# One more step in the ramp of a channel shuffle: tiles of 4, 8, 16, 24 KB a partition instead of 4, 8, 16, and 12 KB last instead of 4

## Chip, cores and metric

The kernel runs on one core of one Trainium2 chip. The metric is device time in microseconds. A run's state is fast unless it is over 1.5% above the fastest run of the same kernel; all comparisons below are between fast runs.

## The reference

```python
batch, h, w, c = 16, 64, 64, 256;  groups = 8
x = x.reshape(batch, h, w, groups, c // groups)
x = x.transpose(0, 1, 2, 4, 3)
x = x.reshape(batch, h, w, c)          # float32
```

Within each run of 256 channels an 8 x 32 matrix is transposed. Nothing is calculated: 67.1 MB are read and 67.1 MB are written.

## The kernel before

```python
_SIZES = [4, 8, 16] + [32] * 15 + [4]     # pixels a partition; one pixel is 1 KB
_IN_BUFS = 3
_OUT_BUFS = 3
...
first = 0
for q in _SIZES:
    in_tile = in_pool.tile([P, biggest * c], F32, name="in_tile")
    nc.sync.dma_start(out=in_tile[:, : q * c], in_=rows(x_flat, first, q))
    out_tile = out_pool.tile([P, biggest * c], F32, name="out_tile")
    nc.vector.tensor_copy(
        out=out_tile[:, : q * c].rearrange("p (i j g) -> p i j g", j=CPG, g=G),
        in_=in_tile[:, : q * c].rearrange("p (i g j) -> p i j g", g=G, j=CPG),
    )
    nc.scalar.dma_start(out=rows(out_flat, first, q), in_=out_tile[:, : q * c])
    first += P * q
```

A tile of q KB a partition is one contiguous piece of 128 q KB in HBM, one row of q KB for each partition. Loads go out from the sync queue, stores from the scalar queue; VectorE does the shuffle between them. Load number k + 3 is issued when copy k is done, since there are three input buffers.

## Time and profile before

| | before |
|---|---|
| time, median of fast runs | 316.9 us |
| profiled span | 315.2 us |
| DMA engines' packet time | 99.2% of 16 engines' span |
| VectorE busy | 119.9 us, 38% |
| one 32 KB row on one DMA engine | 1213 ns |
| period of a 32 KB tile in the middle | 19.4 us, of which the copy 7.5 |

The prediction below shows the lines that this table comes from. Two more things help to read them. The first is how deep the queues are. The page's DMA issues of the kernel before give output and input, engine, count, KB and the median time from issue to landing:

```profile
in_tile<-in_x_dram SPq DMA_DIRECT2D x15, 4096.0 KB, 50.5
out_dram<-out_tile ACTq DMA_DIRECT2D x15, 4096.0 KB, 42.4
```

A 4 MB transfer takes 8 rows x 1213 ns = 9.7 us of each engine, but lands 50 or 42 us after its issue. The rest is waiting behind other rows. The second is the copy of the first 32 KB tile in the timeline (start, duration, engine, what it does, and in brackets how long the engine had been idle and for what):

```profile
24.38 7.50 DVE L49 COPY out_tile<-in_tile 128x8192 f32<-128x8192 f32 x1 [7.81 <-DMA in_tile<-in_x_dram]
```

VectorE stands idle for 7.81 us where the tiles jump from 16 to 32 KB. This is the gap that the change aims at.

### The profile page before, as it was taken

What the parts mean: (1) busy time and instruction counts of PE and PEld (TensorE: products, weight loads), DVE (VectorE), ACT (ScalarE), POOL (GpSimd) and SP (SyncE); (2) the same over time, 40 slices, a digit from 0 to 9 for tenths busy, and PEclk for the clock granted to TensorE, in tenths of its full rate; (3) what the DMA queues carried; (4) which work ended last, traced back from release to release, by engine and by line L of the source; (5) the groups of instructions that cost most, each with busy time, mean ns of one, the idle gap of its engine ahead of it and who ended that gap; (6) DMA issues with size and microseconds to landing.
All of it is one profiled execution on the core that took longest, in us unless ns stands there. A gap on an engine that the chain in (4) does not pass through costs nothing.

```text
span 315.2 us, 150 instructions
## 1 busy us (share of the span) xinstructions
DVE 119.9 (38%) x19; POOL 0.2 (0%) x4
## 2 busy tenths in 40 slices
DVE  2419270905318062270722608135090440905500
POOL 0000000000000000000000000000000000000000
DMA  8999999999999999999999999999999999999996
GB/s 314 408 422 458 403 449 408 457 408 453 412 453 412 458 412 453 420 445 428 437 428 437 437 428 437 428 437 433 437 433 437 428 441 424 445 420 426 439 441 291
DMA packets 5472, 134.22 MB, mean 426 GB/s; under 512 B 608, under 2 KB 608, under 8 KB 1120
## 3 DMA queue, kind: packets, MB, share of 16 engines
q1 hardware_dynamic: 2736, 67.11, 49.8%
q10 hardware_dynamic: 2736, 67.11, 49.4%
HBM read 67.11 MB, written 67.11 MB: 426 GB/s over the span
## 4 chain that ended last, share of the span: by engine, by line
DMA 40%; another core or an unknown queue 30%; DVE 25%; issue 0%; DVEq 0%; SPq 0%
DMA in_tile<-in_x_dram 40%; DVE out_tile L49 25%; DVEq L49 0%; SPq L47 0%
## 5 line engine op out<-in xcount | busy, mean ns | idle before, releaser
L49 DVE COPY out_tile<-in_tile 128x8192 f32<-128x8192 f32 (+3 forms) x19 | 119.9, 6313 | 179.3 <-DMA in_tile<-in_x_dram 179.3
L71 POOL MEMSET const-uint8-127<- 128x1 uint8 x1 | 0.1, 103 | 0.0
L71 POOL MEMSET const-bfloat16-1.0<- 128x1 bf16 x1 | 0.1, 102 | 0.0
L71 POOL MEMSET const-float32-0.0<- 128x1 f32 x1 | 0.1, 99 | 0.2 <-issue 0.2
L71 POOL MEMSET const-float32-1.0<- 128x1 f32 x1 | 0.1, 99 | 0.0
## 6 DMA issues: line engine op xcount, KB each, us to landing
in_tile<-in_x_dram SPq DMA_DIRECT2D x15, 4096.0 KB, 50.5
out_dram<-out_tile ACTq DMA_DIRECT2D x15, 4096.0 KB, 42.4
in_tile<-in_x_dram SPq DMA_DIRECT2D x1, 2048.0 KB, 11.1
out_dram<-out_tile ACTq DMA_DIRECT2D x1, 2048.0 KB, 30.1
in_tile<-in_x_dram SPq DMA_DIRECT2D x2, 512.0 KB, 22.7
in_tile<-in_x_dram SPq DMA_DIRECT2D x1, 1024.0 KB, 5.5
out_dram<-out_tile ACTq DMA_DIRECT2D x2, 512.0 KB, 14.4
out_dram<-out_tile ACTq DMA_DIRECT2D x1, 1024.0 KB, 22.9
```

Source lines behind the costliest of these rows:

```text
L49: nc.vector.tensor_copy(out=out_tile[:, : q * c].rearrange("p (i j g) -> p i j g", j=CPG, g=G), in_=in_tile[:, : q * c].rearrange("p (i g ...
L71: nc = _bacc.Bacc("TRN2", target_bir_lowering=False, num_devices=1)
```

## The change

The intent: a step of 24 KB between 16 and 32 KB, so that the fourth tile is loaded, copied and stored sooner. To keep the total at 512 KB a partition, one 32 KB tile goes, and the last tile grows from 4 to 12 KB. Nothing else changes, and there are still nineteen tiles.

```diff
-_SIZES = [4, 8, 16] + [32] * 15 + [4]
+_SIZES = [4, 8, 16, 24] + [32] * 14 + [12]
```

## The prediction

> **What bounds the kernel now.** I read the page first: how full the DMA engines are, and what each queue's packets took.
>
> ```profile
> span 315.2 us, 150 instructions
> ...
> DVE 119.9 (38%) x19; POOL 0.2 (0%) x4
> ...
> DMA packets 5472, 134.22 MB, mean 426 GB/s; under 512 B 608, under 2 KB 608, under 8 KB 1120
> ...
> q1 hardware_dynamic: 2736, 67.11, 49.8%
> q10 hardware_dynamic: 2736, 67.11, 49.4%
> ```
>
> The two queues (q1 loads, q10 stores) together fill 49.8 + 49.4 = 99.2% of sixteen engines' span: 0.992 x 315.2 = 312.7 us of packet time per engine. VectorE, the only other worker, is busy 38%. So the engines' packet time is the bound, and what a change can win without cutting it is the other 0.8%, about 2.5 us. The windows say where that sits (columns: stretch and length, VectorE busy, GpSimd busy, clock, DMA share, GB/s; a packet is put wholly into the stretch in which it starts, so a share may pass 1.00).
>
> ```profile
> 0.00:2.00 2.00, 0.00 (x0) 0.20 (x4) 1.00 0.18 29
> 2.00:16.00 14.00, 6.39 (x3) 0.00 (x0) 1.00 1.00 404
> 16.00:32.00 16.00, 8.07 (x2) 0.00 (x0) 1.00 1.04 442
> 32.00:74.00 42.00, 14.89 (x2) 0.00 (x0) 1.00 1.00 431
> 74.00:287.00 213.00, 82.03 (x11) 0.00 (x0) 1.00 1.00 433
> 287.00:312.00 25.00, 8.55 (x2) 0.00 (x0) 1.00 0.99 426
> 312.00:313.90 1.90, 0.00 (x0) 0.00 (x0) 1.00 0.64 261
> 313.90:315.15 1.25, 0.00 (x0) 0.00 (x0) 1.00 0.00 0
> ```
>
> Idle engine time: 2.0 x 0.82 = 1.6 us before the first packet, 1.9 x 0.36 = 0.7 us while the engines finish one by one, 1.25 us after the last packet. In between, through ramp, middle and drain, there is no hole: the share is 0.99 to 1.04 in every stretch. (The three add up to 3.6 us, not 2.5, because neighbouring packet records overlap by a few ns.)
>
> Third, what the change could touch: the copies by shape, and VectorE's waits.
>
> ```profile
> L49 DVE COPY out_tile<-in_tile 128x8192 f32<-128x8192 f32 x15 | 111.9, 7459 | 166.2 <-DMA in_tile<-in_x_dram 166.2
> L49 DVE COPY out_tile<-in_tile 128x4096 f32<-128x4096 f32 x1 | 3.8, 3835 | 4.1 <-DMA in_tile<-in_x_dram 4.1
> L49 DVE COPY out_tile<-in_tile 128x1024 f32<-128x1024 f32 x2 | 2.2, 1099 | 7.6 <-DMA in_tile<-in_x_dram 7.6
> L49 DVE COPY out_tile<-in_tile 128x2048 f32<-128x2048 f32 x1 | 2.0, 2019 | 1.5 <-DMA in_tile<-in_x_dram 1.5
> ```
>
> All of VectorE's idle time waits for loads. The timeline of the end:
>
> ```profile
> 287.23 7.47 DVE L49 COPY out_tile<-in_tile 128x8192 f32<-128x8192 f32 x1 [11.95 <-DMA in_tile<-in_x_dram]
> 294.73 4.92 ACTq L53 DMA_DIRECT2D out_dram<-out_tile  x2
> 298.20 1.09 DVE L49 COPY out_tile<-in_tile 128x1024 f32<-128x1024 f32 x1 [3.50 <-DMA in_tile<-in_x_dram]
> ```
>
> The last copy ends at 299.29 us, but packets run until 313.9: 14.6 us of stores are still queued. The chain of waits stops at that last copy, so the chain isn't what sets the end here; the backlog is.
>
> **What the skill says.** (1) "DMA: Bandwidth & Descriptors", section "Issuing engines are not separate DMA queues": transfers issued from different engines run on the same 16 DMA engines and interleave. The trace agrees: two queues at 49.8% and 49.4%, never both full. (2) Same page, "Queues, rings and completion order": each engine goes round its queues packet by packet. The packet records agree, row by row: over 287 to 297 us one engine alternates a 4 KB load row (159 ns) with a 32 KB store row (1213 ns). (3) Same page, "Where 436 GB/s comes from": a ceiling of 435.2 GB/s. The middle runs at 433, so there is half a per cent to be had by any arrangement of transfers. (4) "SBUF — State Buffer", "SBUF: two separate sides": a compute instruction cannot slow a DMA. The records agree: the 32 KB store rows' median and 95th percentile are both 1213 ns, VectorE busy or not.
>
> **The change, part by part.** Row records by size: 4 KB 159 ns, 8 KB 309, 16 KB 611, 32 KB 1213, and a 9 ns packet for each transfer's semaphore. From 16 to 32 KB that is 602/16 = 37.6 ns a KB, so I put 24 KB at 611 + 8 x 37.6 = 912 ns and 12 KB at 309 + 4 x 37.7 = 460 ns (estimates by interpolation). Each engine moves 8 rows of a tile.
>
> Removed, each direction: one 32 KB tile and one 4 KB tile, 8 x (1213 + 159) = 10.98 us. Added: 24 KB and 12 KB, 8 x (912 + 460) = 10.98 us. Net 0.00. The tiles stay nineteen, the packets 5472, the bytes 134.22 MB.
>
> VectorE: removed 7.46 + 1.10 = 8.56 us. Added, at (7459 - 3835)/16 = 227 ns a KB: 24 KB 3.84 + 1.81 = 5.65, 12 KB 2.02 + 0.91 = 2.93, together 8.58. Net +0.02 us, on an engine with 62% idle.
>
> Ramp: the first three loads are the same, and the fourth is still issued at the end of the first copy, 5.2 us. The 32 KB load landed at 24.3 and its copy ended at 31.9. A 24 KB load has 8 x (1213 - 912) = 2.4 us less ahead of it, so lands near 21.9; its copy of 5.65 ends near 27.6. So fourth store and seventh load go out 4.3 us earlier. Does an engine have nothing else to do in that time? Before, the load of the sixth tile, issued at 16.6, landed only at 54.7, and the third store, issued at 16.6, only at 46.7: both queues hold work past 31.9. An earlier issue only lengthens a queue. Worth 0.
>
> Drain: before the last load can be finished, 8 KB a row less has to be loaded than before, and stores keep pace, so the last 32 KB load lands 2 x 8 rows x 8 KB x 37.6 ns = 4.8 us earlier, 287.15 - 4.8 = 282.3. The last load's 12 KB rows alternate with 32 KB store rows: 8 x (460 + 1213) = 13.4 us (before 8 x (159 + 1213) = 11.0, and the two loads landed 10.9 apart), so it lands near 295.7. Copy 2.93 and about 0.1 of issue: store out near 298.8, about 1.0 us to its first packet (as at the start, 0.73 to 1.76). The queue before it holds stores until 313.9 - 8 x 0.46 = 310.2. Slack 310.2 - 299.8 = 10.4 us, against 313.9 - 1.3 - 300.3 = 12.3 before. Still hidden.
>
> Sum: 0.00 engine time, 0 at the start (same first load), 0 at the end. Span 315.2, time 316.9.
>
> **Rivals.** First: the ramp step pays. If the 4.3 us of earlier store filled a hole, the time would be 316.9 - 4.3 = 312.6, faster by 1.4%. For it: a jump from 16 to 32 KB looks coarse, and VectorE does wait 7.8 and 6.0 us after it. Against: the share in 2 to 32 us is 1.00 to 1.04, so there is no hole; VectorE's idleness costs nothing. Second: the larger last tile is exposed: its copy is 1.8 us longer and its store 8 x (460 - 159) = 2.4 us longer, together +4.2, time 321.1, slower by 1.3%. For it: that is what a last tile does where nothing else is queued, and the chain ends on it. Against: 10.4 us of slack. Third: rows of 24 and 12 KB run worse than interpolated, or the start has more slow packets. In the first 20 us, packet records exceed their usual duration by 0.9 us per engine in all; should the regrouped ramp double or drop this, the time moves by up to 0.9 us either way. If the new sizes were 10% slow, 2 x 10.98 x 0.1 = +2.2 us. No sign of it: cost is linear over the four sizes seen. None of the rivals alone crosses 2% (6.3 us).
>
> **Range and chances.** The best number is the time before, 316.9. Its three runs span 0.7 us (316.57 to 317.26); with the slow packets of the ramp and a small step between sessions I take 0.8 us either side: 316.1 to 317.7. A change over 2% needs a hole that no view shows, or a mechanism that I've not thought of: 1% each way; within 2%, 98%.
>
> **What would show it.** Right: the queues still add up to about 99.2%, packets are 5472, the share in every stretch from 2 to 312 us is 0.99 or more, the fourth copy takes about 5.65 us and ends near 27.6, the last copy takes about 2.9 and ends near 298.7, and packets end near 313.9. Wrong: a stretch in 2 to 32 us under 0.97 (ramp), a last store that lands well after the one ahead of it by more than its own 3.7 us (drain), or 24 KB rows well away from 912 ns (packet cost). A time under 315 or over 319 would mean that the sum of packet time isn't what sets the end.

## The result

The changed kernel takes 316.80 us (316.57 to 316.97, six runs), the kernel before in the same rounds 316.91 us (316.57 to 317.26, six runs). The ratio is 0.9997, with a 95% interval of 0.9984 to 1.001: no difference. Ratios here are the mean time of one kernel's fast runs over that of the other's of the same rounds, so not quite the ratio of the medians quoted.

The page of the changed kernel:

```profile
span 314.8 us, 150 instructions
...
DVE 120.4 (38%) x19; POOL 0.2 (0%) x4
...
DMA packets 5473, 134.22 MB, mean 426 GB/s; under 512 B 609, under 2 KB 609, under 8 KB 865
...
q1 hardware_dynamic: 2736, 67.11, 49.8%
q10 hardware_dynamic: 2736, 67.11, 49.4%
```

The two queues have the same packets, bytes and shares as before. (The one packet more is of a third queue, which fetches instructions.) The windows:

```profile
2.00:16.00 14.00, 6.54 (x3) 0.00 (x0) 1.00 1.00 408
16.00:32.00 16.00, 6.11 (x2) 0.00 (x0) 1.00 1.00 426
32.00:74.00 42.00, 19.52 (x3) 0.00 (x0) 1.00 1.02 437
74.00:287.00 213.00, 82.44 (x12) 0.00 (x0) 1.00 1.00 434
287.00:312.00 25.00, 5.79 (x2) 0.00 (x0) 1.00 0.98 421
```

No hole appeared, none closed. (The trace also has one record for each DMA packet, with its start, duration, size and queue; "packet records" means these. In them the engines are full up to 310 us; the 0.98 comes from rows put into the stretch in which they start.) The copies of the new shapes, and the timelines of ramp and end:

```profile
L49 DVE COPY out_tile<-in_tile 128x6144 f32<-128x6144 f32 x1 | 5.7, 5651 | 5.5 <-DMA in_tile<-in_x_dram 5.5
...
L49 DVE COPY out_tile<-in_tile 128x3072 f32<-128x3072 f32 x1 | 3.0, 2976 | 6.0 <-DMA in_tile<-in_x_dram 6.0
```

```profile
21.98 5.65 DVE L49 COPY out_tile<-in_tile 128x6144 f32<-128x6144 f32 x1 [5.52 <-DMA in_tile<-in_x_dram]
35.52 7.51 DVE L49 COPY out_tile<-in_tile 128x8192 f32<-128x8192 f32 x1 [7.89 <-DMA in_tile<-in_x_dram]
```

```profile
282.39 7.43 DVE L49 COPY out_tile<-in_tile 128x8192 f32<-128x8192 f32 x1 [11.88 <-DMA in_tile<-in_x_dram]
295.79 2.98 DVE L49 COPY out_tile<-in_tile 128x3072 f32<-128x3072 f32 x1 [5.97 <-DMA in_tile<-in_x_dram]
```

The fourth copy ends at 27.6 instead of 31.9 us, and the last copy ends at 298.8 instead of 299.3. VectorE's longest idle stretch in the ramp has moved one tile on (7.89 us ahead of the fifth copy) and isn't shorter. The last packet ends at 313.4 us (before: 313.9). So the intended effect is there, 4.3 us, and the time does not see it.

### The profile page after: what moved, and what is told of

Same layout as the page of the kernel before. It is cut to its first block, busy times and chain, and to the rows that moved or that the text cites. A ratio compares the mean times of both kernels' runs of the same rounds, so it can differ in the third digit from the quotient of the medians.

```text
span 314.8 us, 150 instructions
## 1 busy us (share of the span) xinstructions
DVE 120.4 (38%) x19; POOL 0.2 (0%) x4
## 3 DMA queue, kind: packets, MB, share of 16 engines
q1 hardware_dynamic: 2736, 67.11, 49.8%
q10 hardware_dynamic: 2736, 67.11, 49.4%
## 4 chain that ended last, share of the span: by engine, by line
DMA 44%; another core or an unknown queue 26%; DVE 24%; issue 0%; SPq 0%; DVEq 0%
DMA in_tile<-in_x_dram 44%; DVE out_tile L49 24%; SPq L47 0%; DVEq L49 0%
## 5 line engine op out<-in xcount | busy, mean ns | idle before, releaser
L49 DVE COPY out_tile<-in_tile 128x8192 f32<-128x8192 f32 (+5 forms) x19 | 120.4, 6336 | 178.4 <-DMA in_tile<-in_x_dram 178.4
## 6 DMA issues: line engine op xcount, KB each, us to landing
out_dram<-out_tile ACTq DMA_DIRECT2D x1, 3072.0 KB, 31.9
```

Of the source, the lines that this page charges most:

```text
L49: nc.vector.tensor_copy(out=out_tile[:, : q * c].rearrange("p (i j g) -> p i j g", j=CPG, g=G), in_=in_tile[:, : q * c].rearrange("p (i g ...
```

## The experiments

**Theory:** from about 2 to 310 us every DMA engine always has a row to move; the sum of the row times sets the end, and the change leaves it alone. **Rival 1:** the ramp step gains up to 4.3 us and the larger last tile loses as much. **Rival 2:** VectorE's chain sets the end, and the change happens to be neutral in it.

The diffs are cut to the lines that matter. They are taken against the changed kernel; where only a new `_SIZES` line stands, it replaces the changed kernel's.

### The ramp step alone

```diff
-_SIZES = [4, 8, 16, 24] + [32] * 14 + [12]
+_SIZES = [4, 8, 16, 24] + [32] * 14 + [8, 4]
```

> The ramp step alone: 4, 8, 16, 24 KB, fourteen of 32, then 8 and 4 KB, so the last tile is the old 4 KB. Main theory (the DMA engines are never without work between start and drain, so the sum of row times sets the end): 316.8 us plus at most 0.5 for one more small tile, ratio to before 0.999 to 1.003. Rival that the ramp step gains up to 4.3 us and the larger last tile gives it back: about 312.6 us, ratio 0.986.

Measured: 316.82 us against 316.69, ratio 1.0004 (0.9992 to 1.0017). With the old last tile back (and one tile of 8 KB before it, so twenty tiles), the ramp step still gains nothing.

### The 24 KB tile at the end instead of in the ramp

```diff
-_SIZES = [4, 8, 16, 24] + [32] * 14 + [12]
+_SIZES = [4, 8, 16] + [32] * 14 + [24, 12]
```

> The same nineteen tile sizes as the changed kernel, with the 24 KB tile moved from the ramp to the place before the last: 4, 8, 16, fourteen of 32, 24, 12 KB. Main theory: 316.8 us, ratio 0.998 to 1.002, as the rows are the same and the order doesn't matter. Rival that ramp step and last tile are worth +-4 us and cancel: the ramp gain is taken away and the larger last tile kept, about 321 us, ratio 1.013.

Measured: 316.69 us against 316.69, ratio 0.9999 (0.9985 to 1.0012). The larger last tile without the ramp step costs nothing. With the run before, this rules out rival 1: two parts that are each worth nothing cannot be a gain and a loss that cancel.

### Every copy done twice

```diff
+        for _ in range(2):
             nc.vector.tensor_copy(...)
```

> The changed kernel with every copy done twice, VectorE busy 241 us instead of 120 and a 32 KB copy 15 us against a period of 19.4. Main theory: VectorE is not on the path; 316.8 us, up to 319 because the drain's slack falls (last copy 6 us instead of 3, and the one before it 15 instead of 7.5). Rival that the chain of waits (copies are 24 per cent of it) sets the end: 75 us more, about 390 us.

Measured: 317.02 us, ratio 1.0008 (0.9995 to 1.002). The 32 KB copies of the changed kernel, and of this one:

```profile
L49 DVE COPY out_tile<-in_tile 128x8192 f32<-128x8192 f32 x14 | 104.8, 7484 | 157.4 <-DMA in_tile<-in_x_dram 157.4
```

```profile
L50 DVE COPY out_tile<-in_tile 128x8192 f32<-128x8192 f32 x28 | 209.7, 7491 | 52.6 <-DMA in_tile<-in_x_dram 52.0
```

VectorE's busy time doubled from 120.4 to 240.9 us; its idle time before these copies fell from 157.4 to 52.6 us. It paid from its idleness. Rival 2 is out, though copies make up 24% of the chain of waits. Each copy of that chain is followed by a wait, put down to a load or to "another core or an unknown queue" (26% of the span); such a chain names what the copies wait for, not what a longer copy would cost.

### How much slack has the ramp? The 24 KB copy three and eight times

```diff
+        for _ in range(3 if q == 24 else 1):      # and 8
             nc.vector.tensor_copy(...)
```

> The changed kernel with the copy of its 24 KB tile (the fourth, the one the change put in) done three times: its store and the seventh load go out 11.3 us later, 38.9 instead of 27.6 us. Main theory: the third store occupies the store queue to 42 us and the loads of the fifth and sixth tile the load queue to about 46 us, so no engine runs dry: 316.8 us, ratio 0.998 to 1.003. Rival that the ramp's timing is on the path: up to 328 us.

Measured: 316.68 us against 316.63, ratio 0.9998 (0.9981 to 1.0015). The copy by shape:

```profile
L50 DVE COPY out_tile<-in_tile 128x6144 f32<-128x6144 f32 x3 | 17.0, 5667 | 5.5 <-DMA in_tile<-in_x_dram 5.5
```

The fourth tile was held back by 17.0 - 5.7 = 11.3 us, more than twice what the change had brought it forward, and nothing came of it.

> The same copy done eight times: it ends near 67 us and the seventh load and fourth store reach the engines near 68. Main theory: the two loads still queued are done near 46 us, so the engines stand still for about 22 us and the time grows by that: 337 to 341 us, with a visible hole from 46 to 68 us. If the ramp had no slack at all the growth would be the whole 39.6 us, 356 us; if it grows by nothing, the main theory is wrong.

Measured: 340.27 us, 23.6 more than before (ratio 1.0747). The copy by shape, and the windows with the hole:

```profile
L50 DVE COPY out_tile<-in_tile 128x6144 f32<-128x6144 f32 x8 | 45.7, 5718 | 5.7 <-DMA in_tile<-in_x_dram 5.5
```

```profile
40.00:46.00 6.00, 5.97 (x2) 0.00 (x0) 1.00 1.11 481
46.00:68.00 22.00, 21.90 (x5) 0.00 (x0) 1.00 0.00 0
68.00:74.00 6.00, 6.00 (x2) 0.00 (x0) 1.00 0.92 306
```

The copies added 45.7 - 5.65 = 40.1 us (39.6 was expected); 22 us of DMA idleness followed, and another 1.3 us per engine of slow load rows when work came back (in the packet records, between 60 and 80 us). So a hole does cost its length, and the method would have seen one. The ramp has some 18 us of slack before the engines run dry (40.1 less the hole of 22), or 16.5 by the time (40.1 less the 23.6 that showed, slow rows included).

### How much slack has the end? The last copy four and eight times

```diff
+        for _ in range(4 if q == 12 else 1):      # and 8
             nc.vector.tensor_copy(...)
```

> The changed kernel with the copy of its last tile (12 KB) done four times, 8.9 us longer: the last store is issued near 307.7 and reaches the engines near 308.8, while the store before it keeps them until 309.4 to 309.8. Main theory: hidden, 316.8 us, ratio 0.998 to 1.003. Rival that the last tile's copy and store are exposed (chain of waits ends there): 325.7 us.

Measured: 316.70 us against 316.63, ratio 1.0 (0.9985 to 1.0015). Hidden: 8.9 us of extra copying cost nothing.

> The last copy done eight times, 20.8 us longer. Main theory: the drain's slack is 309.6 minus 299.8, about 9.8 us, so 20.8 - 9.8 = 11.0 us show: 327.8 us (326.5 to 329). Rival that it is exposed from the start: 337.6 us.

Measured: 327.73 us (median; one of four runs, 331.2, lifts the ratio to 1.0375). That is 11.1 us more than the 316.63 us of before. The timeline and the windows of its end:

```profile
295.86 23.91 DVE L50 COPY out_tile<-in_tile 128x3072 f32<-128x3072 f32 x8 [5.82 <-DMA in_tile<-in_x_dram]
```

```profile
300.00:309.00 9.00, 8.90 (x4) 0.00 (x0) 1.00 1.05 451
309.00:321.00 12.00, 10.67 (x4) 0.00 (x0) 1.00 0.04 16
321.00:325.80 4.80, 0.00 (x0) 0.00 (x0) 1.00 0.68 287
```

The copies end 23.91 - 2.98 = 20.9 us later, 11.1 show, so the last tile had 20.9 - 11.1 = 9.8 us of slack behind the stores of the tiles ahead of it.

### No ramp at all: a miss

```diff
-_SIZES = [4, 8, 16, 24] + [32] * 14 + [12]
+_SIZES = [32] * 16
```

> No ramp at all, sixteen tiles of 32 KB. Main theory: the three loads issued at the start are 29 us of work for the engines, the first copy ends near 19.5 us, so no engine runs dry in the ramp; three tiles fewer save about 0.4 us of small packets; the last copy of 7.5 us and its issue eat nearly all of the backlog of one 32 KB store (9.7 us), so up to 1 us may be lost there. 316 to 318 us. Rival that a ramp is needed because the first store waits: the first store goes out near 19.5 instead of 5.2 us, so up to 14 us more, 331 us.

Measured: 324.33 us (323.27 to 325.15) against 316.69, ratio 1.0238 (1.022 to 1.0257). Neither number was right. The windows:

```profile
74.00:287.00 213.00, 81.27 (x11) 0.00 (x0) 1.00 1.00 423
287.00:304.00 17.00, 4.01 (x2) 0.00 (x0) 1.00 1.00 432
304.00:312.00 8.00, 4.57 (x1) 0.00 (x0) 1.00 0.89 381
312.00:320.00 8.00, 0.00 (x0) 0.00 (x0) 1.00 0.84 360
320.00:322.40 2.40, 0.00 (x0) 0.00 (x0) 1.00 0.03 14
```

The missing ramp left no hole: from 3 to 305 us the engines are full. But in the middle they move 423 GB/s instead of 434, at the same share of 1.00. The rows themselves became slower. In the packet records between 74 and 287 us, load rows of 32 KB take 1267 ns on average, up to 2288, while in the fast kernels each takes 1213; store rows stay at 1216. The slow rows come in bursts, nearly all on the first three rows that an engine moves of a load tile (about 30, 257 and 103 ns over on average, counted in order of start; the other five under 8). Beyond the usual durations they add up to 6.6 us per engine (before: 1.3). The engines drift apart as the run goes on: the first load tile lands within 0.6 us on all engines, the last within 4.7 (before: 1.1 at most). This leaves holes at the end: 8 x 0.11 + 8 x 0.16 + 2.4 x 0.97 = 4.5 us idle from 287 us on, against 2.2 before. Together 5.3 + 2.3 - 0.5 (packets of three tiles saved) = 7.1 of the 7.2 us by which this span, 322.4 us, is longer than the 315.2 of before.

What makes the rows slow? Three more kernels were made for three causes: tiles that begin at a multiple of 4 MB in HBM (A), engines kept in step for want of small first tiles (B), and the distance between the load and the store stream (C).

### No small start, other addresses

```diff
+_SIZES = [28] + [32] * 15 + [4]
```

> After the miss of the kernel without a ramp (324.3 us, load rows of 32 KB of up to 1.7 us and more, in bursts on the first three rows of each load tile): what makes these rows slow? Tiles of 28 KB, fifteen of 32, 4 KB last: still no small tiles at the start, but each 32 KB tile now begins 3.5 MB past a multiple of its own 4 MB. Theory A (the start of a tile at a multiple of 4 MB in HBM): the slow rows go, 316 to 317.5 us. Theory B (small tiles at the start put the engines out of step): they stay, 322 to 326 us.

Measured: 324.01 and 324.69 us in the two fast runs, ratio 1.024 (1.022 to 1.0261); the other two, 335 and 340 us, are left out (their clock is 1.00 like that of every run here, so what slowed them isn't known). The middle is slow again:

```profile
74.00:287.00 213.00, 82.54 (x11) 0.00 (x0) 1.00 1.00 425
```

Other addresses don't help, which speaks against A.

### A small start, tiles at multiples of 4 MB

```diff
+_SIZES = [4, 8, 20] + [32] * 15
```

> A ramp of 4, 8 and 20 KB, together 32, then fifteen tiles of 32 KB: small tiles at the start, but each 32 KB tile begins at a multiple of 4 MB. Theory A (address): slow rows at each tile's start, 321 to 326 us. Theory B (ramp puts engines out of step): no slow rows; 316.5 to 318 us (the last tile of 32 KB may show up to 1 us).

Measured: 316.72 us against 316.76, ratio 0.9999 (0.9983 to 1.0016), with a fast middle:

```profile
74.00:287.00 213.00, 82.64 (x11) 0.00 (x0) 1.00 1.00 433
```

Theory A is out.

### No ramp, every copy twice

```diff
+_SIZES = [32] * 16
+        for _ in range(2):
             nc.vector.tensor_copy(...)
```

> Sixteen tiles of 32 KB with every copy done twice: addresses and start as without a ramp, but the first store goes out 7.5 us later, so loads and stores pass through their tiles at another distance from each other (before, a store tile ended 2.9 us after a load tile). Theory C (slow rows come where load and store are at the same place of their tiles): the slow rows go, 316.5 to 318.5 us. Theories A and B: they stay, 322 to 327 us.

Measured: 316.95 us against 316.76, ratio 1.0007 (0.9992 to 1.0022). More VectorE work made the kernel without a ramp 7 us faster, with the same tiles at the same addresses:

```profile
74.00:287.00 213.00, 165.62 (x23) 0.00 (x0) 1.00 1.00 433
```

B, as it stood, falls: there is no small tile here and no slow middle. C stands so far, but not in the words of the expectation, as the table after the next run shows.

### A small start with the distance of the slow kernels

```diff
+_SIZES = [4, 12] + [32] * 15 + [16]
```

> Both slow kernels (no ramp, and no ramp shifted) have large first tiles and also a store tile that ends 2.4 to 2.9 us after a load tile; the fast ones end theirs 8 to 15 us after, or within 1 us of it. To separate the two: tiles of 4 and 12 KB, fifteen of 32, 16 KB last, a small start whose store tiles I estimate to end again about 2.4 us after a load tile (from row times and the 4 us that the first store waited[...]). If the distance decides: slow load rows at each tile's start, 319 to 327 us. If the small start decides (theory B in a new form): no slow rows, 316.3 to 317.3 us. If the distance doesn't come out between 1.5 and 4 us the run tells nothing of this, only whether another ramp is as good.

Measured: 323.45 us (323.04 to 324.27) against 316.73, ratio 1.0224 (1.021 to 1.0238), and the distance came out at 2.4 to 3.1 us, as it had to for the run to count.

```profile
74.00:287.00 213.00, 79.49 (x11) 0.00 (x0) 1.00 1.00 425
```

All kernels by distance, that is by how long after the end of a load tile the next store tile ends, in the middle of the run (means over the sixteen engines, from the small packets with which each engine reports that its part of a tile is done; below zero, the store tile ends first); "slow rows" is what rows took beyond their usual durations, per engine over the whole run:

| kernel | distance, us | slow rows, us | time, us |
|---|---|---|---|
| no ramp, copies twice | -1.1 | 1.9 | 316.95 |
| 24 KB copy eight times | 0.0 | 2.8 | 340.27 (22 us hole) |
| no ramp | 2.4 to 2.9 | 6.6 | 324.33 |
| 28 KB first | 2.4 to 3.1 | 5.8 | 324.0, 324.7 |
| 4 and 12 KB first | 2.4 to 3.1 | 5.6 | 323.45 |
| 4, 8, 20 KB first | 8.2 | 1.5 | 316.72 |
| changed kernel | 9.7 | 1.2 | 316.80 |
| last copy four times | 10.1 | 1.4 | 316.70 |
| before | 10.3 | 1.3 | 316.91 |
| ramp step alone | 10.4 | 1.5 | 316.82 |
| last copy eight times | 10.4 | 1.5 | 327.73 (12 us hole) |
| 24 KB tile at the end | 11.0 | 1.4 | 316.69 |
| 24 KB copy three times | 11.2 | 1.4 | 316.68 |
| copies twice | 15.0 | 1.4 | 317.02 |

The three slow kernels, and only they, have the loads 2.4 to 3.1 us ahead of the stores: one pair of rows, 2 x 1.21 us, as an engine alternates between the queues. At -1.1, at 0 and at 8 us or more the rows are fast, so "at the same place of their tiles" was not the right description; one pair ahead fits. That the distance goes with the slow rows, whatever the first tiles and the addresses are, is shown by these runs; no kernel held one between 0 and 2.4, between 3.1 and 8.2, or above 15 us. The distance also comes first: without a ramp it is 2.4 us from the third load tile on.

A second description fits as well. The same packets give the whole lead, by how much load tile k ends before its own store tile k: 41 to 43 us in the middle of the three slow kernels, 46.9 to 58.2 in all the others (0.0 and -1.1 in the table are leads of 58.2 and 57.0). So the slow kernels are also those with the shortest lead, and no run here separates "one pair ahead" from "a lead of less than some 45 us". Why a load row slows down there, whether by banks of HBM, by something in the DMA engines or otherwise, stays open; no record tells it.

## Why the prediction was right

- **The floor.** The step that carries the prediction, equal row times removed and added, holds: 24 KB rows took 912 ns and 12 KB rows 460 (medians), both as interpolated; the mean of the 24 KB load rows, which lie in the ramp, is 925. The shares of the queues are unchanged.
- **The ramp.** The fourth load, copy and store came out as worked (copy from 21.98 to 27.63, worked 21.9 to 27.6), and "worth 0" was tested: holding the tile back by 11.3 us costs nothing either.
- **The drain.** The last copy was worked to end near 298.7 and ended at 298.77; its slack was worked as 10.4 us and measured as 9.8.
- **The rivals.** The first two fell to their own runs. Of the third, odd row sizes cost nothing, and slow rows of the first 20 us came to 1.0 us instead of 0.9.
- **Two small slips.** The stretch from 287 to 312 us came out at 0.98, under the 0.99 named as a sign, without a hole behind it. And "about 1.0 us to its first packet" holds for engines without work only: while loads are running, the first store of the kernel before was issued at 5.24 and began at 9.21, 4.0 us later. For the last store this is covered by the slack and changed nothing.
- **What it did not see.** It took the durations of rows as given, whatever the order of transfers, and did not ask whether the new order keeps them; in this it had luck. They are as given with the old and the new ramp, whose distances are 10.3 and 9.7 us. A ramp of 4 and 12 KB, which the same working would have called neutral too, costs 2.2%. The chance of 1% for such a thing was too low for a change of this kind; that this change is neutral is no proof that any ramp is.

No variant was clearly faster than either kernel. The fast ones all lie within 0.4 us.

## What to carry to other kernels

Where the DMA engines are full from end to end, ask of a change first whether it alters the sum of their packet times; the gaps of an engine that waits for them are slack, and doubling that engine's work is a cheap test. Then look at GB/s beside the share: a share of 1.00 at 423 instead of 434 GB/s meant rows that took longer, with no engine idle. If tiles or start-up are rearranged, compare the distance between the load and store streams before and after, since here a change of it went with 2% more time without any visible wait.

## What the Trainium skill lacked or had wrong

- No page tells that row times can depend on how far the load stream is ahead of the store stream: with load tiles ending 2.4 to 3.1 us before store tiles (or with a lead of 41 to 43 us; the runs don't separate the two), load rows of 32 KB took up to 2.3 us instead of 1.21, and the whole kernel 2.2 to 2.4% longer, at addresses and tile sizes that were fast with another distance.
- "DMA: Bandwidth & Descriptors", section "Queues, rings and completion order", has an engine drain a packet of about 9 to 17 descriptors before it changes queues. Here the trace counts each row as a packet (19 tiles x 9 x 16 = 2736 a queue, 8 rows and one small packet of a tile on each engine), and the engines changed queue after each: from 287 to 297 us one of them takes a 32 KB store row (1213 ns) and a 4 KB load row (159 ns) in turn.
- The same page, "Latency and other measured facts", gives about 600 ns to the first byte of a transfer issued from the sync or scalar engine. This isn't contradicted: on idle engines the first packet came at 1.76 us, 1.0 after the start of the issuing instruction (0.73) and 0.66 after its end (1.10). What no page has is the case of engines that are at work: the first store's first packet came 4.0 us after the start of its issue before (5.24 to 9.21) and 4.6 without a ramp (20.43 to 25.03), with nothing ahead of it in its own queue. Why is not shown.
